# A hybrid decoder layer on one core: attention moved from the GLU into the out projection, low operands first, and a longer run of weight loads in the down stage

## The chip, the cores and the metric

The kernel runs on one core of a Trainium2 chip. The metric is the device time of one execution in microseconds, taken as the median of several runs. One further execution is profiled; the views of the profile and of its trace all describe that one.

## What is computed

One decoder layer on 256 tokens of width 2048, all in float32. One input projection feeds two groups; their results, side by side, go through one output projection, a norm, a gated feed-forward net and a second norm:

```python
proj = h @ w_in[l]
u_ssm, q, k, v, qi, ki, wi = jnp.split(proj, split_at, axis=-1)
...
y_attn = _dsa_attention(q, k, v, qi, ki, wi)
mix = jnp.concatenate([y_ssm.astype(h.dtype), y_attn.astype(h.dtype)], axis=-1) @ w_out[l]
h = _layer_norm(DEEPNORM_ALPHA * h + mix, ln1_g[l], ln1_b[l])
f = _conv_ffn(h, w_up[l], w_gate[l], conv_w[l], conv_b[l], w_down[l])
h = _layer_norm(DEEPNORM_ALPHA * h + f, ln2_g[l], ln2_b[l])
...
# the end of _s5_mixer, which gives y_ssm
return y * jax.nn.sigmoid(y @ w_glu + b_glu)
...
# in _conv_ffn, with h = x @ w_up and hp its padded copy
hc = conv_b + sum(conv_w[i] * hp[:, i:i + seq] for i in range(CONV_WIDTH))
return (jax.nn.gelu(hc, approximate=False) * (x @ w_gate)) @ w_down
```

`w_out` is 2048 x 2048, `w_up` and `w_gate` are 2048 x 5632, `w_down` is 5632 x 2048.

The attention has 8 query heads of 128 in two groups of four, each group with one key and value head. An indexer scores all earlier tokens for each query, and only the 64 best are attended; in the kernel this is a mask that is added to the scores. Tokens come in two blocks of 128, so a block has 128 or 256 keys to look at.

## The kernel before

**Products.** Each float32 operand is split into a high part, in the format fp32r, and a low rest. ACT copies a weight into `wh` (L133) and DVE subtracts to get `wl` (L136); `split` does the same for activations (L181, L182). A product is then three: high by high, low by high, high by low (`mm3`, L186 to L188). The up and gate products use `wide_half` (L206): high and low part of the activation stand side by side, so a pass with a high weight has 512 columns and one with a low weight 256.

**Weights.** The list `order` names all weight blocks in the order of their use; each is loaded as two halves of 128x1024 (512 KB). `load` sends a half on SP's queue into one of three `raw` buffers, `fetch` issues its two copies into one of four `wh` and four `wl` buffers, and `next_half` keeps `state["ahead"]` halves fetched ahead of the one in use (four as a rule). Halves that are listed in `special` have buffers of their own, so that the queue can run further ahead; they are used from the third column block of the out projection on (`halves_before_db2`) and for the last 20 halves of the down products (`spare2`).

**Order.** The program is written once; a scheduler places independent instructions, except in `manual_schedule` stretches, which keep the written order on the engines that they name. Generators that are registered with `add_bg` are advanced by `pump` after each product group, so their work is spread among the products. ACT's functions that need a table go through `in_turn` (L175), which keeps them in written order.

**Stages around the change**, with the times of the trace. The eight GLU tiles (24 products each, over 8 blocks of the contraction) run to 278 us. Each writes one of four PSUM banks (`o00` to `o11`), and ACT's sigmoid must read a bank before the fifth tile after it can be written. `attention(0)`, the first four heads, is pumped beside the last projections and the GLU: scores (L720), mask and scaling on DVE (L724), their maximum (L726), exponentials on ACT (L175), normalisation (L734), transposes on TensorE (L740), a copy on ACT (L743), the product with the values (L747), and a split. Scores, transposes and value products share two PSUM buffers, `misc`. `attention(1)` is pumped into the out projection.

The out projection contracts 16 blocks into four column blocks `db` of 512. Blocks 0 to 7 of `mix` come from the GLU, 8 to 11 from `attention(0)`, 12 to 15 from `attention(1)`. It takes `db` 0 and 1 with the first half of `mix`, then both with the second half, then `db` 2 whole; `db` 3 follows in a hand-written stretch with the first norm, whose 32 transposes (L875) stand among its products. The up and gate stage (44 tiles, products from 401.5 us) comes next, then the down stage: 44 row blocks `f`, two halves each, twelve products per half, into eight accumulators. The last five row blocks (LAG = 5) are collected and used column block by column block, so their ten halves must all be there; `state["ahead"]` is raised to ten at `f == NF - 2 * LAG`, f = 34. The activations of a row block are split just ahead of its use (`act_split`), with seven buffers.

Of the kernel before, what the change touches and what calls it, by code (L numbers as in the profile page):

```python
# [10 lines left out]
F32 = mybir.dt.float32  # L11
# [71 lines left out]
def block_kernel(ctx: ExitStack, tc: tile.TileContext, x_t, x_n, prm_d, cst_d, ssm_d, w_in_d, w_kw_d, w_v_d,  # L83
# [17 lines left out]
    order += [w_out_d[i] for i in (0, 1, 4, 5, 2, 3, 6, 7, 8, 9, 10, 11, 12, 13, 14, 15)]  # L101
# [5 lines left out]
    for n, src in enumerate(order):  # L107
        if n == 41:
            halves_before_db2 = len(halves)
        w = src.shape[1]  # L110
        halves += [src[:, :w // 2], src[:, w // 2:]]
# [82 lines left out]
    def wide_half(out, half, tiles, kh):  # L194
# [7 lines left out]
        steps = list(passes(0)) + list(passes(1))  # L202
        if kh:
            steps.append(steps.pop(7))
# [501 lines left out]


    def attention(c):
        qs = qt[4 * c:4 * c + 4]
        for b in range(2):  # L710
            w = 128 * (b + 1)
            e4 = post.tile([P, 4, S], F32, name="e4", bufs=2)
            mx = post.tile([P, 4], F32, name="mx", bufs=2)
            sm = post.tile([P, 4], F32, name="sm", bufs=2)
            nh = 512 // w
            for g0 in range(0, 4, nh):
                lp = misc_tile()
                for g in range(g0, g0 + nh):
                    o = lp[:, (g - g0) * w:(g - g0 + 1) * w]
                    T.matmul(o, lhsT=qs[g][:, b * 128:(b + 1) * 128], rhs=kt_[c][:, 0:w], start=True, stop=True)  # L720
                    yield
                for g in range(g0, g0 + nh):
                    hd = c * 4 + g
                    V.scalar_tensor_tensor(e4[:, g, :w], lp[:, (g - g0) * w:(g - g0 + 1) * w], SCALE * 2.0 ** (hd + 1),  # L724
                                           nm[b][:, :w], op0=ALU.mult, op1=ALU.add)
            V.tensor_reduce(mx, e4[:, :, :w], axis=AX.X, op=ALU.max)  # L726
            V.tensor_tensor(mx, mx, cc("nslope")[:, c * 4:c * 4 + 4], op=ALU.mult)
            for g in range(4):
                in_turn(e4[:, g, :w], e4[:, g, :w], AF.Exp, scale=2.0 ** -(c * 4 + g + 1), bias=mx[:, g:g + 1],
                             accum_out=sm[:, g:g + 1])  # L730
            rs = post.tile([P, 4], F32, name="rs", bufs=2)
            V.reciprocal(rs, sm)
            for g in range(4):
                V.tensor_scalar(e4[:, g, :w], e4[:, g, :w], rs[:, g:g + 1], None, op0=ALU.mult)  # L734
            yield
            pt = []
            for sb in range(b + 1):
                tp = misc_tile()
                for g in range(4):
                    T.transpose(tp[:, g * 128:(g + 1) * 128], e4[:, g, sb * 128:(sb + 1) * 128], ident)  # L740
                    yield
                t = post.tile([P, 512], F32, name="pt", bufs=3)
                A.activation(t, tp, AF.Copy)  # L743
                pt.append(t)
# [478 lines left out]
```

## Time and profile before

| | |
|---|---|
| three runs | 1144.85, 1138.44, 1144.31 us (median 1144.31) |
| profiled execution, device time | 1139.62 us |
| its span in the profile | 1137.8 us, mean granted clock 0.984 |
| PE (matmul) busy | 1097.6 us, 96% |
| DVE busy | 748.2 us, 66% |
| ACT busy | 563.7 us, 50% |
| weights read | 200 MB, 178 GB/s over the span |

Engines are PE (TensorE), DVE (VectorE), ACT (ScalarE), POOL and SP, whose queue issues the loads. Times count from the start of the span. The granted clock is the share of TensorE's 2.4 GHz that it was allowed to run at: 1.00 is full, 0.50 is 1.2 GHz.

### The profile page before, as it was taken

The numbers are of one execution on the slowest core, as the hardware profiler recorded it, in microseconds if no ns is written. First come the engines' busy times: TensorE is split into PE (matmuls) and PEld (weight loads), VectorE is DVE, ScalarE is ACT, GpSimd is POOL, SyncE is SP. The second block draws the span as 40 slices with busy tenths as digits, with TensorE's granted clock in tenths as the row PEclk, the third lists the DMA queues.
The fourth block names the chain that finished last, engine by engine and source line by source line (L and its number), as shares of the span: only waits on it lengthen the run. The fifth ranks groups of instructions, "written<-read, shape, count | busy, mean of one in ns | idle before, by whom it ended". The sixth has DMA issues, their size and how long they took to land.

```text
span 1137.8 us, 16797 instructions
## 1 busy us (share of the span) xinstructions
PE 1097.6 (96%) x6576; PEld 945.3 (83%) x6576; DVE 748.2 (66%) x1052; ACT 563.7 (50%) x813; POOL 0.2 (0%) x4
## 2 busy tenths in 40 slices
PE   8999999877999999999999999999999999999975
PEld 7998999767878888888888888888888888888864
DVE  7979998785666756677666565666565544444557
ACT  5865436445554755555444555545555444444430
POOL 0000000000000000000000000000000000000000
PEclk9999999988999999999999999999999999999988
DMA  8753444323566375555755555555554655555632
GB/s 267 237 167 115 159 145 145 139 74 108 207 212 214 104 259 192 185 185 187 262 194 190 189 189 187 192 187 187 185 188 165 216 189 186 186 188 190 212 130 74
DMA packets 59310, 204.44 MB, mean 180 GB/s; under 512 B 7264, under 2 KB 10080, under 8 KB 58592
## 3 DMA queue, kind: packets, MB, share of 16 engines
q1 hardware_dynamic: 59232, 203.38, 52.8%
q8 instruction: 51, 0.84, 0.3%
q14 instruction: 27, 0.22, 0.1%
HBM read 200.20 MB, written 2.10 MB: 178 GB/s over the span
## 4 chain that ended last, share of the span: by engine, by line
PE 86%; DMA 6%; DVE 3%; ACT 2%; issue 1%; SPq 1%; DVEq 0%; ACTq 0%
PE pd L206 41%; PE e L186 6%; PE e L188 6%; PE e L187 6%; PE acc L188 4%; PE acc L186 4%; PE acc L187 4%; DMA raw<-in_w_down_dram 3%; PE o L188 3%; PE o L187 3%; PE o L186 3%; DMA raw<-in_w_in_dram 1%; PE misc L599 1%; PE bu L556 1%; DVE wl L136 1%
## 5 line engine op out<-in xcount | busy, mean ns | idle before, releaser
L136 DVE TENSOR_TENSOR wl<-raw,wh 128x1024 fp32r<-128x1024 f32 x333 | 406.8, 1223 | 309.9 <-ACT wh L133 308.5
L133 ACT ACTIVATE wh<-raw 128x1024 fp32r<-128x1024 f32 x333 | 352.1, 1058 | 339.4 <-PE pd L206 141.5
L206 PE MATMUL pd<-mix,wh 128*128 128x512 f32 x1344 | 337.7, 393 | 0.7 <-ACT gate L1005 0.7
L206 PEld LDWEIGHTS pd<-mix,wh 128*128 128x128 f32 x1344 | 241.5, 189 | 44.0 <-ACT gate L1005 1.1
L206 PEld LDWEIGHTS pd<-mix,wl 128*128 128x128 f32 x1344 | 183.3, 190 | 13.1
L206 PE MATMUL pd<-mix,wl 128*128 128x256 f32 x1344 | 187.4, 282 | 0.0
L186 PE MATMUL e<-wh,acth 128*128 128x512 f32 x304 | 120.6, 397 | 5.5 <-ACT wh L133 5.5
L187 PE MATMUL e<-wh,actl 128*128 128x512 f32 x304 | 120.3, 396 | 0.0
L188 PE MATMUL e<-wl,acth 128*128 128x512 f32 x304 | 119.6, 396 | 0.5 <-DVE wl L136 0.5
L186 PE MATMUL acc<-x,wh 128*128 128x256 f32 (+1 forms) x400 | 113.9, 285 | 1.4 <-ACT x L181 1.2
L187 PE MATMUL acc<-x,wl 128*128 128x256 f32 (+1 forms) x400 | 114.2, 286 | 0.7 <-DVE wl L136 0.5
L188 PE MATMUL acc<-x,wh 128*128 128x256 f32 (+1 forms) x400 | 114.1, 285 | 0.8 <-DVE x L182 0.8
L186 PEld LDWEIGHTS acc<-x,wh 128*128 128x128 f32 (+1 forms) x400 | 75.8, 190 | 3.1 <-ACT x L181 1.4
L187 PEld LDWEIGHTS acc<-x,wl 128*128 128x128 f32 (+1 forms) x400 | 75.8, 190 | 2.2 <-DVE wl L136 0.7
L188 PEld LDWEIGHTS acc<-x,wh 128*128 128x128 f32 (+1 forms) x400 | 75.9, 190 | 2.1 <-DVE x L182 1.0
L186 PEld LDWEIGHTS e<-wh,acth 128*128 128x128 f32 x304 | 57.1, 188 | 20.0 <-ACT wh L133 6.2
L188 PEld LDWEIGHTS e<-wl,acth 128*128 128x128 f32 x304 | 57.1, 188 | 15.0 <-DVE wl L136 1.0
L187 PEld LDWEIGHTS e<-wh,actl 128*128 128x128 f32 x304 | 57.1, 188 | 13.8
L175 ACT ACTIVATE hc<-hc 128x256 f32<-128x256 f32 x44 | 18.4, 417 | 69.8 <-DVE hc L1046 69.8
L1033 DVE TENSOR_TENSOR sum<-sum,pd 128x256 f32<-128x256 f32 x84 | 34.9, 415 | 0.0
L188 PE MATMUL o<-wl,mix 128*128 128x512 f32 x80 | 31.9, 398 | 0.0
L186 PE MATMUL o<-wh,mix 128*128 128x512 f32 x80 | 31.6, 397 | 0.0
(262 smaller groups left out, 1201.7 us busy)
## 6 DMA issues: line engine op xcount, KB each, us to landing
raw<-in_w_gate_dram SPq DMA_DIRECT2D x88, 512.0 KB, 4.1
raw<-in_w_up_dram SPq DMA_DIRECT2D x88, 512.0 KB, 4.1
raw<-in_w_down_dram SPq DMA_DIRECT2D x88, 512.0 KB, 3.7
raw<-in_w_in_dram SPq DMA_DIRECT2D x51, 512.0 KB, 4.1
raw<-in_w_out_dram SPq DMA_DIRECT2D x32, 512.0 KB, 4.6
raw<-in_w_glu_dram SPq DMA_DIRECT2D x8, 512.0 KB, 3.8
raw<-in_w_v_dram SPq DMA_DIRECT2D x4, 512.0 KB, 4.5
z<-in_x_n_dram SPq DMA_DIRECT2D x1, 2048.0 KB, 8.8
```

The costliest lines, as they stand in the source:

```text
L133: A.activation(h[:, :w], raw[:, :w], AF.Copy)
L136: V.tensor_sub(l[:, :w], raw[:, :w], h[:, :w].bitcast(F32))
L175: ins = A.activation(*args, **kw)
L186: T.matmul(out, lhsT=lh[0], rhs=rh[0], start=start, stop=False)
L187: T.matmul(out, lhsT=lh[1], rhs=rh[0], start=False, stop=False)
L188: return T.matmul(out, lhsT=lh[0], rhs=rh[1], start=False, stop=stop).ins
L206: ins = T.matmul(out[:, 0] if low else out, lhsT=w, rhs=r, start=kh == 0 and i == 0, stop=kh == 1 and i == 15)
L556: T.matmul(bu[:, sd, ri, k:k + 128], lhsT=bt[r, 2 * bi + c_, h, ri, :], rhs=ustk[r, c_, h, :], start=True, stop=True)
L599: T.matmul(yp[32 * q:32 * q + 32, c_, e, k1:], lhsT=cbd[k1 * 2 + ri][:, ct * 4 + q, :], rhs=hv[ri][:, q % 2, k:k + 128 - k1], start=False, ...
L1033: V.tensor_tensor(t, t, p[:, 0], op=ALU.add)
```

## The change

There are three parts.

*GLU first.* `attention(0)` leaves the background of the GLU. The attention is now a class with four steps: `scores`, `weights` (exponentials, reciprocal, normalisation), `turn` (transposes and their copies) and `values` (products with the values, and the split into `mix`), and there are four chains: `a00` and `a10` for the first token block of either group of heads, `a01` and `a11` for the second. Only the scores of `a00` and `a10` stand among the GLU tiles; the first two GLU tiles are interleaved. The out projection takes three column blocks at once, in three phases over the contraction, so 24 units (a unit is the six products of one half with one token block) come ahead of the first that reads an attention result. TensorE's order there is written by hand: the table `beside` says ahead of which unit each step of the attention stands. The third column block accumulates in two banks that are free then.

*Low operands.* In `wide_half`, the second half of each tile takes its eight low passes first and its eight high passes after them.

*Ten buffers through down.* The queue may run ten halves ahead from f = 4 on. Special buffers are listed for the last 80 halves; two of each ten live in `hl2` and `hl3`, four in a new pool. The activations are split in groups of four row blocks into `hl0` and `hl1`.

```diff
-    order += [w_out_d[i] for i in (0, 1, 4, 5, 2, 3, 6, 7, 8, 9, 10, 11, 12, 13, 14, 15)]
+    order += [w_out_d[i] for i in (0, 1, 4, 5, 8, 9, 2, 6, 10, 3, 7, 11, 12, 13, 14, 15)]
...
-        steps = list(passes(0)) + list(passes(1))
-        if kh:
-            steps.append(steps.pop(7))
+        steps = list(passes(1)) + list(passes(0)) if kh else list(passes(0)) + list(passes(1))
...
+    class Attend:
+        def scores(self):
...
+            self.e4 = e4 = post.tile([P, 4, w], F32, name=f"e4{b}", bufs=2)
+            self.mx = mx = post.tile([P, 4], F32, name="mx", bufs=4)
...
+        def weights(self):
...
+        def turn(self):
...
+        def values(self):
...
+    a00, a10, a01, a11 = (Attend(c, b) for b in range(2) for c in range(2))
...
-    def beside_q():
-        yield from glu_in()
-        yield from attention(0)
-
-    add_bg(beside_q(), 1)
+    add_bg(glu_in(), 1)
...
+    first_glu = [(glu_acc(nt), next_half()) for nt in range(2)]
+    for some in (range(6), range(6, 8)):
+        for acc, half in first_glu:
+            glu_products(acc, half, some)
+    for nt in range(8):
...
+        sgm = post.tile([P, S], F32, name="sgm", bufs=2)
+        in_turn(sgm, acc[:, :S], AF.Sigmoid, bias=pc("bglu", nt))
...
+        if nt == 3:
+            a00.scores()
+        if nt == 4:
+            a10.scores()
...
-    add_bg(attention(1), 2)
...
-                t = post.tile([P, 4, 128], F32, name="h1f", bufs=2)
+                t = post.tile([P, 4, 128], F32, name="h1f", tag="pt", bufs=3)
...
-    for db, some in ((0, range(4)), (1, range(4)), (0, range(4, 8)), (1, range(4, 8)), (2, range(8))):
...
+    oacc = [row_banks(0), row_banks(1), [acc_tile() for _ in range(2)], None]
+    a00.weights()
+    a10.weights()
+    beside = {2: a01.scores, 3: a01.weights, 6: a00.turn, 7: a10.turn, 9: a00.values, 10: a10.values,
+              11: a11.scores, 12: a11.weights, 14: a01.turn, 17: a01.values, 22: a11.turn, 25: a11.values}
+    unit = 0
+    with tc.manual_schedule(engines={mybir.EngineType.PE}):
+        for some in (range(4), range(4, 6), range(6, 8)):
...
+            for db in range(3):
+                for i in some:
+                    half = next_half()
+                    for b in range(2):
+                        beside.get(unit, lambda: None)()
+                        rows_half(oacc[db][b], mix, 2 * i, half, b, 16)
+                        unit += 1
...
-        if i < 4:
+        if i < 2:
...
-    for i in range(4 * LAG):
+    for i in range(16 * LAG):
         if i % (2 * LAG) < 2 * LAG - 4:
-            special[len(halves) - 4 * LAG + i] = spare2(i % (2 * LAG))
+            special[len(halves) - 16 * LAG + i] = spare2(i % (2 * LAG))
...
     def act_split(f):
-        h = ff.tile([P, S], F32R, name="acth", bufs=LAG + 2)
-        l = ff.tile([P, S], F32R, name="actl", bufs=LAG + 2)
+        if f < 1:
+            h, l = (ff.tile([P, S], F32R, name=f"act{n}{f}") for n in "hl")
+        else:
+            slot, place = (f - 1) // 4, (f - 1) % 4
+            if place == 0:
+                parts[slot] = ahl.tile([P, 4, 2, S], F32R, name="acthl", tag=f"hl{slot % 2}")
+            h, l = (parts[slot][:, place, i] for i in range(2))
...
-        if f == NF - 2 * LAG:
+        if f == NF - 8 * LAG:
             state["ahead"] = 2 * LAG
```

Where this moves instructions, engine by engine. ACT in the later part of the GLU, before: weight copies (`wh`), the softmax of the second token block (`e4` by exponentials, with `sm` their sums) and the first sigmoid (`sgm`), which reads the accumulator `glu`.

```order
L133 ACTIVATE wh_3005<-raw_3003 128x1024
L133 ACTIVATE wh_3041<-raw_3039 128x1024
L743 ACTIVATE pt_2703<-misc_2678 128x512
L133 ACTIVATE wh_3077<-raw_3075 128x1024
L181 ACTIVATE mixh_2572<-misc_2705 128x4x128
L175 ACTIVATE e4_2715,sm_2717<-e4_2715,mx_2716 128x256 x4
L175 ACT_TABLE_LOAD
L175 ACTIVATE sgm_2961<-glu_2930,prm_70 128x256
```

The same place in the changed kernel:

```order
L133 ACTIVATE wh_3011<-raw_3009 128x1024
L133 ACTIVATE wh_3060<-raw_3058 128x1024
L175 ACTIVATE sgm_2954<-glu_2923,prm_70 128x256
L175 ACTIVATE sgm_2990<-glu_2959,prm_70 128x256
L133 ACTIVATE wh_3096<-raw_3094 128x1024
L133 ACTIVATE wh_3132<-raw_3130 128x1024
L181 ACTIVATE mix0_2847<-sgm_2954 128x256
L181 ACTIVATE mix0_2847<-sgm_2990 128x256
L133 ACTIVATE wh_3210<-raw_3208 128x1024
L175 ACTIVATE sgm_3039<-glu_3008,prm_70 128x256
```

The exponentials no longer stand ahead of the sigmoids; the third sigmoid (`sgm_2954`) now stands behind the weight copy `wh_3060`, and the fifth (`sgm_3039`) behind `wh_3210`.

DVE at the end of the attention's second block, before: maximum `mx`, reciprocal `rs` and normalisation of `e4`, then the sigmoids' products with y (`sgm`, L790) and their splits (`mix0`).

```order
L726 TENSOR_REDUCE mx_2716<-e4_2715 128x4
L727 TENSOR_TENSOR mx_2716<-mx_2716,cst_71 128x4
L732 RECIPROCAL rs_2746<-sm_2717 128x4
L734 TENSOR_SCALAR e4_2715<-e4_2715,rs_2746 128x256 x4
L790 TENSOR_TENSOR sgm_2961<-sgm_2961,y0_1087 128x256
L790 TENSOR_TENSOR sgm_2997<-sgm_2997,y1_1089 128x256
L182 TENSOR_TENSOR mix0_2926<-sgm_2961,mix0_2926 128x256
```

In the changed kernel DVE comes to the first normalisations at the start of the out projection (`e41` are scores of the second token block, `e40` the weights of the first; `mix1` the last GLU splits):

```order
L721 SCALAR_TENSOR_TENSOR e41_3232<-misc_3234,nm1_1901 128x256 x2
L721 SCALAR_TENSOR_TENSOR e41_3232<-misc_3239,nm1_1901 128x256 x2
L733 RECIPROCAL rs_3189<-sm_3184 128x4
L723 TENSOR_REDUCE mx_3233<-e41_3232 128x4
L733 RECIPROCAL rs_3200<-sm_3195 128x4
L735 TENSOR_SCALAR e40_2995<-e40_2995,rs_3189 128x128 x4
L182 TENSOR_TENSOR mix1_2848<-sgm_3124,mix1_2848 128x256
L182 TENSOR_TENSOR mix1_2848<-sgm_3160,mix1_2848 128x256
L724 TENSOR_TENSOR mx_3233<-mx_3233,cst_71 128x4
L735 TENSOR_SCALAR e40_3044<-e40_3044,rs_3200 128x128 x4
```

The scores of the second block and the last two products of the GLU now stand ahead of the first normalisation, and both reciprocals stand ahead of it too.

ACT toward the end of the down stage, before: a weight copy for each half and the split `acth` of one row block after about every second copy; the special buffers `wx` begin here.

```order
L133 ACTIVATE wh_9772<-raw_9770 128x1024
L133 ACTIVATE wh_9794<-raw_9792 128x1024
L181 ACTIVATE acth_10056<-act_4203 128x256
L133 ACTIVATE wh_9812<-raw_9810 128x1024
L133 ACTIVATE wx_9852<-raw_9850 128x1024
L133 ACTIVATE wh_9834<-raw_9832 128x1024
L181 ACTIVATE acth_10096<-act_4203 128x256
L133 ACTIVATE wx_9873<-raw_9871 128x1024
L133 ACTIVATE wx_9890<-raw_9888 128x1024
L181 ACTIVATE acth_10136<-act_4203 128x256
L133 ACTIVATE wx_9911<-raw_9909 128x1024
```

ACT in the same stage of the changed kernel:

```order
L181 ACTIVATE acthl_9840<-act_4209 128x256 x4
L133 ACTIVATE wx_9712<-raw_9710 128x1024
L133 ACTIVATE wx_9731<-raw_9729 128x1024
L133 ACTIVATE wxh2_9748<-raw_9746 128x1024
L133 ACTIVATE wxh3_9768<-raw_9766 128x1024
L133 ACTIVATE wxh4_9786<-raw_9784 128x1024
L133 ACTIVATE wxh5_9806<-raw_9804 128x1024
L133 ACTIVATE wh_9824<-raw_9822 128x1024
L133 ACTIVATE wh_9845<-raw_9843 128x1024
L181 ACTIVATE acthl_9991<-act_4209 128x256 x4
```

The splits stand in groups of four (`acthl`), and eight weight copies, six of them into special buffers, stand between two groups.

## Rows read from the trace of the kernel before

**Rows 1.** The page: busy time of each engine; shares of the last chain.

```profile
PE 1097.6 (96%) x6576; PEld 945.3 (83%) x6576; DVE 748.2 (66%) x1052; ACT 563.7 (50%) x813; POOL 0.2 (0%) x4
...
PE 86%; DMA 6%; DVE 3%; ACT 2%; issue 1%; SPq 1%; DVEq 0%; ACTq 0%
```

**Rows 2.** Windows: length, busy PE, PEld, DVE, ACT, POOL, granted clock, DMA share, GB/s.

```profile
240.00:260.00 20.00, 9.11 (x58) 7.25 (x56) 16.09 (x43) 9.38 (x21) 0.00 (x0) 0.82 0.30 105
370.00:392.00 22.00, 21.93 (x111) 17.66 (x111) 17.16 (x33) 17.28 (x37) 0.00 (x0) 1.00 0.34 117
1080.00:1100.00 20.00, 13.98 (x57) 10.46 (x56) 10.68 (x11) 9.25 (x11) 0.00 (x0) 0.89 0.56 187
```

**Rows 3.** PE's waits in 200 to 330: us in total, times, longest.

```profile
PE glu L186 <- ACT sgm L175: 9.9, 1, 9.9
...
PE misc L720 <- DVE mixl L182: 2.0, 1, 2.0
```

**Rows 4.** Timeline of ACT around 240 to 262: start, us, what, idle before.

```profile
240.96 1.06 ACT L133 ACTIVATE wh<-raw 128x1024 fp32r<-128x1024 f32 x1 [3.95 <-PE glu L188]
242.03 1.28 ACT L175 ACT_TABLE_LOAD   x1
...
243.73 0.39 ACT L175 ACTIVATE e<-e,mx 128x128 f32<-128x128 f32 x1
...
258.54 0.51 ACT L175 ACTIVATE e<-e,mx 128x256 f32<-128x256 f32 x1 [9.37 <-DVE mx L727]
...
261.93 0.47 ACT L175 ACTIVATE sgm<-glu,prm 128x256 f32<-128x256 f32 x1
```

**Rows 5.** Windows through the first hole.

```profile
245.00:252.50 7.50, 4.03 (x16) 2.29 (x14) 7.41 (x20) 3.91 (x5) 0.00 (x0) 1.00 0.50 175
252.50:262.50 10.00, 0.13 (x2) 0.04 (x1) 7.01 (x21) 3.93 (x11) 0.00 (x0) 0.51 0.16 59
262.50:266.30 3.80, 3.80 (x18) 3.80 (x19) 3.09 (x8) 2.67 (x7) 0.00 (x0) 0.50 0.00 0
```

**Rows 6.** PE's waits in 1040 to 1130.

```profile
PE e L186 <- ACT wh L133: 5.5, 2, 4.8
```

**Rows 7.** The last chain in 1040 to 1137.8: start, us, piece.

```profile
1052.41 1.24 DVE wx L136
...
1067.09 3.64 DMA raw<-in_w_down_dram
...
1073.16 6.95 DMA raw<-in_w_down_dram
```

**Rows 8.** Windows through the second hole.

```profile
1092.00:1099.60 7.60, 1.58 (x6) 0.51 (x4) 3.15 (x4) 3.11 (x3) 0.00 (x0) 0.74 0.62 208
1099.60:1102.50 2.90, 2.90 (x7) 2.33 (x8) 2.41 (x2) 1.06 (x1) 0.00 (x0) 0.50 0.00 0
```

**Rows 9.** Timeline of PE from the last GLU products to the first out products.

```profile
277.71 0.28 PE L188 MATMUL glu<-yl,wh 128*128 128x256 f32 x1
...
278.06 0.28 PE L188 MATMUL glu<-yl,wh 128*128 128x256 f32 x1
278.18 0.39 PE L186 MATMUL o<-wh,mix 128*128 128x512 f32 x1
278.41 0.40 PE L187 MATMUL o<-wh,mix 128*128 128x512 f32 x1
```

**Rows 10.** Timeline of DVE around 245.

```profile
245.49 0.86 DVE L734 TENSOR_SCALAR e<-e,rs 128x128 f32<-128x128 f32 x4
```

**Rows 11.** The page, DMA issues: count, KB each, median us to landing.

```profile
raw<-in_w_down_dram SPq DMA_DIRECT2D x88, 512.0 KB, 3.7
...
raw<-in_w_out_dram SPq DMA_DIRECT2D x32, 512.0 KB, 4.6
...
z<-in_x_n_dram SPq DMA_DIRECT2D x1, 2048.0 KB, 8.8
```

**Rows 12.** Groups of instructions by line and form, PE in 237 to 402.

```profile
L875 PE MATMUL misc<-cst,z 128*128 128x128 f32 x32 | 4.6, 275 | 0.1
```

More of the change, by code (lines that the diff above doesn't have):

```diff
@@ L107, in block_kernel @@
     for n, src in enumerate(order):
-        if n == 41:
-            halves_before_db2 = len(halves)
+        if n == 42:
+            halves_before_spare = len(halves)
         w = src.shape[1]
@@ L704, in block_kernel, with __init__ @@
     post = pre.enter_context(pool("post"))
[L708 to L714, printed above, removed]
+    class Attend:
+        def __init__(self, c, b):
+            self.c, self.b, self.w = c, b, 128 * (b + 1)
+        def scores(self):
+            c, b, w = self.c, self.b, self.w
+            self.e4 = e4 = post.tile([P, 4, w], F32, name=f"e4{b}", bufs=2)
+            self.mx = mx = post.tile([P, 4], F32, name="mx", bufs=4)
             nh = 512 // w
@@ L894, in spare @@
                 lambda: proj.tile([P, 1024], F32R, name="wql", tag=("qi1", "q1")[n]))
-    first = halves_before_db2
-    for i in range(24):
+    first = halves_before_spare
+    for i in range(22):
         if i % 11 < 7:
             special[first + i] = spare(i)
-    oacc = {}
     def rows_half(out, tiles, kt0, half, b, n):
@@ L913, in row_banks @@
         return [pso.tile([P, 512], F32, name=f"o{i}{b}") for b in range(2)]
-    for db, some in ((0, range(4)), (1, range(4)), (0, range(4, 8)), (1, range(4, 8)), (2, range(8))):
-        if 4 in some:
-            drain()
-            if db == 0:
+    oacc = [row_banks(0), row_banks(1), [acc_tile() for _ in range(2)], None]
[6 more added lines that the diff above has]
+        for some in (range(4), range(4, 6), range(6, 8)):
+            if 6 in some:
                 root_ready(post)
@@ L923, in block_kernel @@
                     nc.sync.dma_start(out=ln10[:, i], in_=ln_d[i:i + 1, :512].broadcast_to([P, 512]))
-        if db == 2:
-            state["ahead"] = 10
-        if some[0] == 0:
-            oacc[db] = row_banks(db % 2)
-        for i in some:
-            half = next_half()
-            for b in range(2):
-                rows_half(oacc[db][b], mix, 2 * i, half, b, 16)
-        if 7 in some:
-            for b in range(2):
-                residual(b, db, oacc[db][b])
+                state["ahead"] = 10
+            for db in range(3):
[5 more added lines that the diff above has]
+                        unit += 1
+                if 7 in some:
+                    for b in range(2):
+                        residual(b, db, oacc[db][b])
     oacc[3], gacc = row_banks(1), row_banks(0)
@@ L1008, in block_kernel @@
     pre.close()
+    wx2 = ctx.enter_context(pool("wx2"))
     ff = ctx.enter_context(pool("ff"))
```

68 lines of the change are left out of this document (33 added, 35 removed).

## Prediction

> **What bounds the kernel now.** The page comes first. TensorE is busy 96% of the span, and 86% of the chain that ended last is its own work [rows 1]. A gain must therefore come from stretches in which TensorE has nothing to do or runs at the lower of its two clocks. Windows of some 20 us find them: 9.1 us busy at a granted clock of 0.82 in 240 to 260, 14.0 at 0.89 in 1080 to 1100, while a window in the middle, 370 to 392, is full at 1.00 [rows 2]. That is the whole case: two holes and a dense rest.
>
> The list of waits names what ends the first hole: 9.9 us for a sigmoid, and before it 2.0 for a split of the attention [rows 3]. The timeline of ACT says why. After the attention's last copy ACT stands idle for 9.37 us, until DVE has the scores' maximum; the exponentials run at 258.54, and the first sigmoid of the GLU waits behind them until 261.93 [rows 4]. The fifth GLU tile needs the PSUM bank which that sigmoid reads. Narrow windows size the hole: 4.03 of 7.5 us busy, then 0.13 of 10, which is 13.3 us idle, and behind it 3.8 us of GLU products at a clock of 0.50 [rows 5], which cost 1.9. **First hole: 13.3 + 1.9 = 15.2 us.**
>
> The second hole is a wait for `wh` in the down products, 5.5 us [rows 6]. The chain there alternates between landings of `w_down` halves and their two copies [rows 7]: ten halves are wanted almost at once for the last five row blocks, and the queue had only ten row blocks to run ahead. Windows give 1.58 us busy of 7.6, then 2.9 us of products at 0.50 [rows 8], which cost 1.45. **Second hole: 6.0 + 1.45 = 7.45 us.**
>
> **The change part by part.** *GLU first.* Up to 237.1 TensorE's list is the same; from there the attention of the first head group no longer stands inside the GLU. No product is added or removed: its 68 products still run, now inside the out projection. So all that changes is waiting, and I count the waits that the new lists make, with durations of before. A GLU product (256 columns) starts every 0.117 us (three in 0.35), an out product (512) every 0.23 [rows 9], so a GLU tile of 24 takes 2.8 us and one unit (six products of a half with one token block) 1.4. The parts of the walk: `wh` copy 1.06, table load 1.28, exponentials 0.39 each, sigmoid 0.47 [rows 4], `wl` 1.24 [rows 7], normalisation of four heads 0.86 [rows 10].
>
> Wait 1. The first four sigmoids no longer wait for an exponential: `wh` of the fifth tile starts at 240.96 as before, the table is in at 243.3, the first sigmoid done at 243.8. The fifth and sixth tile find their banks free; 109 of their products are left at 237.1 (12.8 us), eight score products stand among them (0.9), and they end at 250.8. The seventh needs the third sigmoid, which ACT holds behind `wh_3060`. That copy's load is sent when the sixth tile's `wl` is done: `wh` at 244.8, `wl` at 246.0, then 3.7 to 4.6 us of landing [rows 11], 1.06 and 0.47. The sigmoid is done at 251.3 to 252.1: wait 0.5 to 1.3, I take 0.9.
>
> Wait 2. The first out product writes the bank of the fifth tile, whose sigmoid ACT holds behind `wh_3210`. That copy takes the buffer of the eighth tile, so it starts only when the GLU ends. 1.06 + 0.47 and two hand-overs: 1.7 (bounds 1.5 and 2.0).
>
> Wait 3. `a00.turn` stands six units and one set of scores (0.9) after the first out product: 9.3 us. ACT has by then `wh_3228`, which waits two units for its buffer (2.8 + 1.06), two sigmoids (0.9), the table (1.28) and eight exponentials (3.1): 9.2. DVE takes both reciprocals ahead of the first normalisation (0.86): 10.4 with hand-overs. Wait 1.1 (bounds 0, since the units may start late, and 2.3, one more `wl`).
>
> Wait 4. `a11.scores` stands one unit behind `a10.values`, and its second tile takes the PSUM buffer that the split of those values must leave. In before the same pair cost 2.0 [rows 3]; bounds 0 and 2.0, I take 0.5, as a whole unit now lies between. The other places (turns at units 14 and 22, values at 9, 10, 17, 25) have three units or more behind their softmax, and wait 0.
>
> Sum of new waits 4.2 us; the clock should hold, none being near the 9.9 that preceded the fall. **First hole: 15.2 − 4.2 = 11.0 us gained.**
>
> *Three column blocks.* 24 units lie ahead of the first one that reads the attention (unit 24), 33 us; the weights arrive in the new order of the list, as many as before. One half serves 2.8 us. A raw buffer is held for a landing of 4.6 [rows 11] and two copies of 1.06 and 1.24, with three buffers 2.3 us per half, so it is covered; if that cover were gone, each half would cost 4.1 (9 to 15 halves until the spare buffers start). Loading `z` (8.8 us to landing [rows 11]) stands on SP's queue ahead of the sixth out half, which is wanted 14 us after; hidden.
>
> *Low operands.* In the second half of each up or gate tile the eight low passes go before the eight high ones. A pass costs what its own columns cost, whichever came before: 0.117 us between two of 256 columns, 0.12 from one of 256 to one of 512, 0.23 behind that [rows 9]. The sum does not change: 0 us, with 84 tiles and a border worth at most 0.02 us each way, ±1.7. `wl` of an odd half is wanted 1.6 us sooner; four buffers of 2.8 us cover that.
>
> *Ten buffers through down.* The queue may run ten halves ahead from f = 4, not from f = 34. One half is used in 2.8 us (twelve products), while a raw buffer's round is 3.64 + 1.06 + 1.24 at best, 2.0 us per half with three of them [rows 4, 7]. Six halves of lead (16.8 us) need about 21 halves at a gain of 0.8; there are 70. The activations now take `hl0` and `hl1` in groups of four: each group waits for the group two before it, on ACT ahead of the weight copies. Only the first groups press: `hl0` is read last 2.8 us before the up stage ends, and f = 1 is wanted 5.6 us after, 8.4 us for at most seven splits of under 0.5 (a sigmoid of the same 128x256 takes 0.47). Nothing waits: **7.45 us gained**. The range of this term is 0 to 7.45.
>
> Sum: 11.0 + 7.45 = 18.5 us, from the profiled execution's 1139.6 to 1121.1. Of the runs shown two lie at about 1144.5 and one at 1138.4, so the profiled one is 4.7 under the median; the same gain from the median gives 1125.8, from the lowest run 1120. I say 1122.
>
> **The rivals.** *Late at set places.* TensorE's list is fixed in the out projection, so any late softmax blocks the products behind it. In 245 to 252.5 three waits of the attention cost 3.5 us [rows 5], 1.15 each; if six more places wait so, that is 6.9 us, and one more fall of the clock 1.9: 1130. For it: DVE is 7.41 of 7.5 us busy there [rows 5]. Against: it has 33 us for that work.
>
> *Loads do not get ahead.* At the end of before a landing took 6.95 us [rows 7]; with the copies that is 9.3, 3.1 us per half with three buffers, and the lead never grows. The second hole stays: 1128.6. Against: the median landing of `w_down` is 3.7 [rows 11].
>
> *Nothing waits.* All four new waits vanish, since the lists absorb them: 1139.6 − 22.7 = 1117.
>
> *Slower.* TensorE drops to 1.2 GHz among the set places and stays. A product then takes 0.41 us (seven in 2.9 [rows 8]), not 0.23: 1.1 us per unit. Twenty-six units reach to the last set place; at 17 of them the gain of 18.5 is gone, and at 26 the time is 1121 + 28 = 1149. For it: the clock fell twice behind waits (to 0.51 in 252.5 to 262.5 [rows 5], 0.74 on average in 1092 to 1099.6 [rows 8]). Against: in 370 to 392, where the norm turns its rows by fp32 transposes among the products, the clock is 1.00 [rows 2, 12]. The Trainium skill bears on this: "TensorE: Matmul & The Clock Gate", section "Part 4: PE-mode transpose", says that transposes do not count as activity for the clock, which would put the stretch with the turns at the lower level; the trace of the norm's 32 transposes does not agree, so I leave this case a small chance.
>
> **How the numbers follow.** Forecast (1117.5 to 1127) 0.62, nothing waits 0.10, late at set places 0.13, loads not ahead 0.05, slower 0.04, both holes half left (about 1136) 0.06. The range leaves out the last two and reaches from 1117 less the spread of a run and the 1.7 of the borders, 1113, to 1130 plus 3 for a run near the median, 1133. About 1% is what a measurement here can tell from no change, so the bound is 1133: faster 0.84, same 0.12, slower 0.04.
>
> **What would show it.** Right: no wait of TensorE over 2.5 us between 237 and 300, the first up product near 390 instead of 401.5, the pause of down gone, the interval of up products unchanged. Wrong: a wait for `e40` or `e41` of several us, a granted clock below 1.00 between 250 and 300, or `wh` waits in the last five row blocks.

## The result, and the profile after

| | before | changed |
|---|---|---|
| runs | 1144.85, 1138.44, 1144.31, 1140.73 us | 1111.4, 1112.53, 1108.79, 1110.82 us |
| median | 1142.52 us | 1111.11 us |
| span of the profiled execution | 1137.8 us | 1109.5 us |

The ratio is 0.9727, with a 95% interval of 0.9691 to 0.9763: faster by some 31 us, where 20 were forecast (1122 against 1142.5), and below the lower end of the range, 1113. The two profiled executions differ by 28.3 us, where 18.5 were worked out. The direction was right; the size was not.

The first thing to do with such a miss is to split it by stage. These times are read from the starts and ends of the products in the two traces:

| stage | before | changed | difference | forecast |
|---|---|---|---|---|
| to the first GLU product (same program) | 228.55 | 231.19 | +2.64 | 0 |
| first GLU product to first up product | 172.94 | 158.42 | −14.52 | −11.0 |
| up and gate, to the first down product | 470.32 | 468.74 | −1.58 | 0 |
| down, to the end of the last product | 254.50 | 239.67 | −14.83 | −7.45 |
| last norm and store | 11.51 | 11.52 | 0 | 0 |

The first line is scatter: over the thirteen profiled executions of this study, with the same order of TensorE's work up to there, the first GLU product starts between 228.55 and 234.12. So the miss lies in the down stage above all.

The page of the changed kernel, as [rows 1] of before:

```profile
PE 1084.8 (98%) x6576; PEld 944.1 (85%) x6576; DVE 747.0 (67%) x1052; ACT 561.0 (51%) x812; POOL 0.2 (0%) x4
...
PE 93%; DMA 2%; DVE 2%; ACT 1%; SPq 1%; issue 1%; DVEq 0%; ACTq 0%
```

TensorE went from 96 to 98% of the span, which is the two holes. But its busy time also fell, from 1097.6 to 1084.8 us, with the same 6576 products. Idle time that goes can't do that. The two stretches at the lower clock behind the holes, which are gone too, explain 3.3 us of the 12.8 [rows 5, 8]; for the rest, the products themselves take less.

The changed kernel's longest waits after the first GLU product, over the whole span (in total, times, longest), to be laid beside [rows 3, 6]:

```profile
PE o L186 <- ACT sgm L175: 2.6, 1, 2.6
...
PE pd L204 <- ACT gate L1021: 0.7, 1, 0.7
PE misc L887 <- issue: 0.6, 1, 0.6
```

The 9.9 for a sigmoid and the 5.5 for `wh` are gone. Of the four new waits one is there, the second. The windows around it (length, busy PE, PEld, DVE, ACT, POOL, granted clock, DMA share, GB/s), beside [rows 5]:

```profile
245.00:259.40 14.40, 14.40 (x123) 14.20 (x122) 13.71 (x33) 9.54 (x15) 0.00 (x0) 1.00 0.55 182
259.40:262.03 2.63, 0.00 (x0) 0.00 (x1) 1.96 (x5) 1.47 (x3) 0.00 (x0) 1.00 0.79 238
262.03:268.03 6.00, 6.00 (x27) 5.05 (x28) 5.59 (x15) 4.29 (x8) 0.00 (x0) 1.00 0.88 337
262.10:275.00 12.90, 12.90 (x61) 10.78 (x62) 12.10 (x35) 11.19 (x32) 0.00 (x0) 1.00 0.70 277
```

The GLU runs without a gap, then 2.63 us are idle, then all is dense at full clock, the turns included.

Now the down stage, in a window where neither kernel waits: before, then changed.

```profile
900.00:1000.00 100.00, 100.00 (x430) 80.31 (x429) 50.08 (x54) 43.47 (x54) 0.00 (x0) 1.00 0.54 189
```

```profile
900.00:1000.00 100.00, 100.00 (x443) 82.81 (x442) 58.06 (x63) 50.66 (x63) 0.00 (x0) 1.00 0.67 223
```

Both are busy for all of 100 us at a clock of 1.00, yet one starts 430 products and the other 443. The timelines of PE show the same over twelve products each, before and then changed:

```profile
900.03 0.39 PE L187 MATMUL e<-wh,actl 128*128 128x512 f32 x1
...
902.83 0.39 PE L187 MATMUL e<-wh,actl 128*128 128x512 f32 x1
```

```profile
900.21 0.39 PE L187 MATMUL e<-wh,acthl 128*128 128x512 f32 x1
...
902.93 0.39 PE L187 MATMUL e<-wh,acthl 128*128 128x512 f32 x1
```

2.80 us against 2.72, so 0.2333 us a product against 0.2267. Over the 1056 products of the stage that is about 7 us, nearly the whole miss of this stage (14.83 against 7.45). "0.23 us" in the prediction had rounded this away.

A clue to its cause is in the changed kernel itself. Its 24 products of the first row block, whose activations lie in a buffer of their own, start every 0.233 us; from the second row block on, with `acthl` in `hl0` and `hl1`, it is 0.227. The built program says where each buffer lies. Before, the split activations lie 224 bytes further, modulo 512, than the weight buffers `wh` and `wl`; `acthl` lies at the same place modulo 512. In each pair of products the one reads its moving operand (the weights here) while the stationary operand of the next (the activations) is loaded, as the busy PEld beside the busy PE shows. That gave the theory of the experiments: the interval hangs on the distance of these two.

### The profile page after: what moved, and what is told of

It is laid out like the page before. It is cut to its first block, busy times and chain, and to the rows that moved or that the text cites. A ratio compares the mean times of both kernels' runs of the same rounds, so it can differ in the third digit from the quotient of the medians.

```text
span 1109.5 us, 16801 instructions
## 1 busy us (share of the span) xinstructions
PE 1084.8 (98%) x6576; PEld 944.1 (85%) x6576; DVE 747.0 (67%) x1052; ACT 561.0 (51%) x812; POOL 0.2 (0%) x4
## 4 chain that ended last, share of the span: by engine, by line
PE 93%; DMA 2%; DVE 2%; ACT 1%; SPq 1%; issue 1%; DVEq 0%; ACTq 0%
PE pd L204 42%; PE e L186 7%; PE e L188 7%; PE e L187 7%; PE acc L188 5%; PE acc L186 5%; PE acc L187 5%; PE o L186 3%; PE o L188 3%; PE o L187 3%; PE misc L653 1%; PE misc L597 1%; PE bu L554 1%; DVE wl L136 1%; DMA xraw<-in_x_t_dram 1%
## 5 line engine op out<-in xcount | busy, mean ns | idle before, releaser
L136 DVE TENSOR_TENSOR wl<-raw,wh 128x1024 fp32r<-128x1024 f32 x299 | 364.7, 1221 | 247.6 <-ACT wh L133 244.1
L133 ACT ACTIVATE wh<-raw 128x1024 fp32r<-128x1024 f32 x299 | 315.7, 1057 | 271.8 <-PE pd L204 136.3
L204 PE MATMUL pd<-mix,wh 128*128 128x512 f32 x1344 | 321.4, 391 | 0.7 <-ACT gate L1021 0.7
L204 PE MATMUL pd<-mix,wl 128*128 128x256 f32 x1344 | 174.8, 283 | 0.0
L136 DVE TENSOR_TENSOR wxl<-raw,wxh 128x1024 fp32r<-128x1024 f32 x42 | 51.4, 1225 | 43.9 <-ACT wxh L133 42.3
L133 ACT ACTIVATE wxh<-raw 128x1024 fp32r<-128x1024 f32 x42 | 44.6, 1061 | 54.3 <-DMA raw<-in_w_down_dram 20.4
L187 PE MATMUL e<-wh,acthl 128*128 128x512 f32 x152 | 59.1, 389 | 0.0
L186 PE MATMUL e<-wh,acthl 128*128 128x512 f32 x152 | 59.0, 389 | 0.0
L188 PE MATMUL e<-wl,acthl 128*128 128x512 f32 x152 | 58.3, 389 | 0.0
L186 PE MATMUL e<-wxh,acthl 128*128 128x512 f32 x128 | 49.8, 389 | 0.0
L187 PE MATMUL e<-wxh,acthl 128*128 128x512 f32 x128 | 49.8, 389 | 0.0
L188 PE MATMUL e<-wxl,acthl 128*128 128x512 f32 x128 | 49.8, 389 | 0.0
```

What stands on the lines that cost most here:

```text
L133: A.activation(h[:, :w], raw[:, :w], AF.Copy)
L136: V.tensor_sub(l[:, :w], raw[:, :w], h[:, :w].bitcast(F32))
L186: T.matmul(out, lhsT=lh[0], rhs=rh[0], start=start, stop=False)
L187: T.matmul(out, lhsT=lh[1], rhs=rh[0], start=False, stop=False)
L188: return T.matmul(out, lhsT=lh[0], rhs=rh[1], start=False, stop=stop).ins
L204: ins = T.matmul(out[:, 0] if low else out, lhsT=w, rhs=r, start=kh == 0 and i == 0, stop=kh == 1 and i == 15)
```

## Experiments

**Each part alone.** The first three runs take the parts of the change apart. The first is the changed kernel with the old `wide_half` and the old down stage (`spare2`, its list and `act_split` as before):

```diff
-        steps = list(passes(1)) + list(passes(0)) if kh else list(passes(0)) + list(passes(1))
+        steps = list(passes(0)) + list(passes(1))
+        if kh:
+            steps.append(steps.pop(7))
...
-        if f == NF - 8 * LAG:
+        if f == NF - 2 * LAG:
```

> The first part of the change alone: the kernel before with the GLU first and the attention in four chains, the up, gate and down stages as before. Theory (the three parts add up, each in its own stage): from the first GLU product to the first up product 158.4 us as in the changed kernel, against 172.9 before, so 13 to 14.5 us less, near 1126; the down products still start every 0.2333 us on average and still pause for about 6 us near the end. Rival (the down stage is shorter because the stages ahead of it end earlier or leave the buffers free sooner): the down stage shrinks from 254.5 us here as well.

Measured: 1125.85 us (median of 4), ratio 0.987 [0.9839, 0.9901]. First GLU product to first up product 159.2 us, down stage 252.8, up and gate 470.3. The down products keep their old interval and wait once, in the list of PE's waits:

```profile
PE e L186 <- ACT wh L133: 3.6, 1, 3.6
```

So the attention's part acts in its own stage alone; that the products of down come closer together because of earlier stages is ruled out. The pause itself differs between executions: by the starts of the products, the waits and the stretch at the lower clock behind them cost 8.2 us in the profiled before, 6.5 here and 6.2 in the next run, which has the old down stage too. The stage from the first GLU product to the first up product took 171.2 to 172.9 us in the five executions with the old attention (mean 171.9), and 158.4 to 161.7 in the five with the new lists as they are (mean 159.7). That is 12 us, with the single pair 14.5, where 11.0 were forecast.

The second part alone, in the kernel before:

```diff
-        steps = list(passes(0)) + list(passes(1))
-        if kh:
-            steps.append(steps.pop(7))
+        steps = list(passes(1)) + list(passes(0)) if kh else list(passes(0)) + list(passes(1))
```

> The second part alone: low passes first in the second half of each up or gate tile. Theory (a change from low to high passes costs products that start late, and a tile now has one such change instead of two): the sum of the 32 intervals of a tile goes from 5.587 us to 5.567, 1.7 us over 84 tiles, with the five intervals behind a low pass at 0.233, 0.236, 0.228, 0.233 and 0.231 us and the others at 0.227. Rival (the 1.6 us by which the up stage of the changed kernel is shorter come from other placements of its buffers): the sum stays at 5.587.

Measured: 1137.0 us, one run, inside the 1136.0 to 1142.35 of the runs of before beside it, so the time alone shows nothing. The trace does. The up and gate stage took 468.7 us instead of 470.3, and a tile 5.567 instead of 5.587. The intervals of a tile, read from the starts in the trace (mean over 76 tiles, us):

```
                              before                       low passes first in the second half
first half, 8 high            .2358 .2283 .2325 .2308      .2267 x8
                              .2267 x4
            8 low             .1133 .1192 .1200 x6         .1133 .1192 .1200 x6
second half                   .2333 .2358 .2283 .2325      8 low:  .1200 x8
                              .2308 .2267 x2 (7 high)      8 high: .2333 .2358 .2283 .2325
                              .1133 .1192 .1200 x6 (low)           .2308 .2267 x3
                              .2333 (1 high)
```

A high pass behind a low one opens five late intervals, 0.027 us together; a low pass behind a high one gives 0.008 back. Before, each tile has two of either, now one. 0.020 us by 84 tiles is 1.7.

The third part with its new places undone:

```diff
-    for i in range(4 * LAG):
+    for i in range(16 * LAG):
         if i % (2 * LAG) < 2 * LAG - 4:
-            special[len(halves) - 4 * LAG + i] = spare2(i % (2 * LAG))
+            special[len(halves) - 16 * LAG + i] = spare2(i % (2 * LAG))
...
-        if f == NF - 2 * LAG:
+        if f == NF - 8 * LAG:
```

> The third part without its new places: the kernel before, with the queue ten halves ahead from the fourth row block on and the list of special buffers over the last 80 halves; the split activations and the special buffers stay where they were. Theory (two things shortened the down stage: the pause, and the interval of the products, which hangs on where the split activations lie): the pause goes, the interval stays at 0.2333 us, the down stage takes 254.5 - 7.45 = 247 us and the kernel 7 to 8 us less. Rival (the loads that run further ahead make the products start closer together): interval 0.2267, the down stage 240 us, 14 to 15 us less.

Measured: 1130.13 us, ratio 0.9919 [0.9888, 0.9949]. No wait of TensorE is left in the down stage, and it took 245.6 us: 8.9 less than the profiled before, 7.7 less than the mean of the three executions with the old down stage (254.5, 252.8, 252.6). Of either, 0.7 us comes from the products that start sooner, the rest is the pause. The window of 900 to 1000, beside the two above:

```profile
900.00:1000.00 100.00, 100.00 (x433) 80.74 (x432) 56.06 (x59) 49.61 (x61) 0.00 (x0) 1.00 0.66 218
```

433 products, not 443: loads that run ahead do not bring the products closer. The three above 430 come from the halves in the two special buffers that lie in the activations' own pool, at distance 0; behind six products of that kind the interval is 0.2269, and with the other halves 0.2333.

**The place of the activations alone.** Before with one unused piece of memory, nothing else:

```diff
+    ff.tile([P, 72], F32, name="shift")
+
     def act_split(f):
```

> The kernel before with one unused piece of 288 bytes ahead of the buffers of the split activations and nothing else. It moves them, and two of the special weight buffers, from 288 bytes above a multiple of 512 to 64 above one, which is where the weight buffers lie. Theory (a product starts later when the stationary operand that is loaded next and the moving operand that is read meanwhile lie at different places modulo 512 bytes): the down products start every 0.2267 us instead of 0.2333, the stage takes 6.9 us less, the pause stays. Rivals (that high and low part share one tile, or lie in the region of the old activations, or that the loads run ahead): no change, 254.5 us for the stage.

Measured: 1132.9 us, ratio 0.9952 [0.9925, 0.9979]. The same window:

```profile
900.00:1000.00 100.00, 100.00 (x443) 82.81 (x442) 51.30 (x56) 44.43 (x55) 0.00 (x0) 1.00 0.60 195
```

443, as in the changed kernel, with the old buffers, the old run of loads and two tiles for high and low part. The stage takes 245.4 us, and the pause is still there, though shorter:

```profile
PE e L186 <- ACT wh L133: 2.7, 2, 2.2
PE e L188 <- DVE wl L136: 0.5, 1, 0.5
```

Of the 9.1 us that the stage is shorter than in the profiled before, 2.4 are this shorter pause (5.8 us with its lower clock, against 8.2) and 6.7 the interval. This settles that the place makes the interval. The kernel gained 6.8 us by the medians from 288 bytes that nobody writes.

**Which distance counts.** Seven buffers at seven distances:

```diff
-        h = ff.tile([P, S], F32R, name="acth", bufs=LAG + 2)
-        l = ff.tile([P, S], F32R, name="actl", bufs=LAG + 2)
+        s = f % 7
+        if f < 7:
+            ff.tile([P, (288, 32, 32, 64, 64, 64, 128)[s] // 4], F32, name=f"shift{s}")
+        h = ff.tile([P, S], F32R, name=f"acth{s}x", bufs=1)
+        l = ff.tile([P, S], F32R, name=f"actl{s}x", bufs=1)
```

> The kernel before with a buffer of its own for the activations of every seventh row block of the down stage, at seven distances from the weight buffers: 0, 32, 64, 128, 192, 256 and 384 bytes modulo 512 (high and low part alike). Theory (only the same place modulo 512 is fast): row blocks of the first distance have products every 0.2267 us, all others 0.2333. Rivals: the same place modulo 256 (then 256 is fast as well), modulo 128 (then 128, 256 and 384 too), or modulo 64 (then all but 32). The mean over the seven tells how many are fast: 0.2323, 0.2314, 0.2295 and 0.2276 us in this order.

Measured: 1137.2 us, one run. The mean interval of the down products by distance, behind at least six products at the same distance (so that late intervals of a change of place are left out):

```
distance, bytes modulo 512     0     32     64    128    192    256    384
products                     101     84    107    108     90     90     90
interval, us               .2267  .2333  .2333  .2320  .2289  .2267  .2327
```

The theory was wrong in its modulus: 256 is as good as 0. The values between are not all alike, and 192 lies between the two levels. What stays is 0 modulo 256, among the distances tried; why 256 is not shown.

**Another stage, another operand.** If the distance counts, moving all activations against the weights must cost in the up stage too, where the activation is the moving operand.

```diff
+    gap = ctx.enter_context(pool("gap"))
+    gap.tile([P, 64], F32, name="shift")
     ahl = ctx.enter_context(pool("ahl"))
```

> The changed kernel with an unused piece of 256 bytes ahead of the pool that holds the activations of every stage. They all move by 256 against `wh` and `wl`; the special buffers of the down stage, which lie behind that pool, move with them. Theory (the distance modulo 512 counts, in every stage): down products with a half in `wh` or `wl` start every 0.2333 us, those with a half in a special buffer every 0.2267, in the same stage; up and gate products, whose moving operand is the activation, gain up to 16 times 0.0067 us a tile, 9 us over the stage (5.567 to 5.67 us a tile); the kernel gets 9 to 15 us slower than the changed one, near 1122. Rival (only the stage with split activations as stationary operand minds, or 256 is as good as 0): the up stage stays at 5.567 us a tile, and the time within 4 us of 1111.

> The changed kernel with an unused piece of 32 bytes, not 256, ahead of the pool that holds the activations of every stage. Seven places and the shift by 256 left a distance of 0 modulo 256 as the fast one. Theory (that distance counts for every product of 512 columns, whichever operand is the activation): down products with a half in `wh` or `wl` start every 0.2333 us and those with a half in a special buffer every 0.2267 (456 and 576 of 1032, so 3.0 us more for the stage); the up and gate stage, all of whose halves lie in `wh` and `wl`, goes from 5.567 us a tile to at most 5.67, up to 9 us more; the kernel lies near 1123. Rival (it counts only where the activation is the stationary operand): the down stage is 3.0 us longer, the up stage stays, the kernel lies near 1114.

Measured: 1114.62 us with 256 bytes, 1117.77 with 32 (the same edit with `[P, 8]`), where 1122 and 1123 were expected. The windows of the up stage and of the down stage, first the changed kernel's up stage, then both with 256 bytes, then both with 32:

```profile
500.00:800.00 300.00, 300.00 (x1726) 265.08 (x1725) 186.41 (x249) 152.76 (x216) 0.00 (x0) 1.00 0.59 197
```

```profile
500.00:800.00 300.00, 300.00 (x1726) 265.09 (x1726) 186.15 (x250) 153.29 (x216) 0.00 (x0) 1.00 0.61 196
900.00:1000.00 100.00, 100.00 (x443) 82.81 (x442) 58.15 (x63) 50.60 (x62) 0.00 (x0) 1.00 0.67 223
```

```profile
500.00:800.00 300.00, 300.00 (x1719) 260.83 (x1718) 186.65 (x249) 152.13 (x215) 0.00 (x0) 1.00 0.60 195
900.00:1000.00 100.00, 100.00 (x436) 81.68 (x436) 55.64 (x58) 48.00 (x57) 0.00 (x0) 1.00 0.66 218
```

With 256 bytes nothing moves in either stage (the changed kernel has 1726 and 443), which fits the seven places and refutes what I expected of that run; both stages take the same in the two profiled executions (468.7 and 239.7 us), and the 3.5 us between the medians are less than the changed kernel's own runs differ by (1108.79 to 1117.78). With 32 both stages slow down. The down stage is 3.3 us longer (3.0 expected): its products with `wh` and `wl` take 0.2333, those with the special buffers, which moved along, 0.2267, with the activations at one and the same place for both. So the distance counts, and not the place of the activations by itself. In the up stage the high passes take 0.2333 on average, whichever came before, as the theory says, but the low passes fall from 0.120 to 0.117, so that a tile costs 5.600, not 5.67, and the stage 2.7 us, not up to 9. So the distance counts whichever operand is the activation; for passes of 256 columns it does something else, which stays open.

That the moving operand is to be compared with the stationary operand of the next product, not with its own, is seen where a distance of 0 goes over into one of 32. In the seven places the stationary operand changes its place there, and the very first interval is late: 0.235 us, the mean of five such changes. In the run with 32 bytes the moving operand changes its place instead; the first interval is still 0.227, and the second is 0.234, the mean of seven.

**The wait that is left.** Ahead of the first out product the changed kernel's ACT does this (timeline: start, us, what, idle before):

```profile
257.64 1.06 ACT L133 ACTIVATE wh<-raw 128x1024 fp32r<-128x1024 f32 x1 [1.87 <-DMA raw<-in_w_out_dram]
...
260.56 1.06 ACT L133 ACTIVATE wh<-raw 128x1024 fp32r<-128x1024 f32 x1 [1.24 <-DMA raw<-in_w_out_dram]
261.52 0.82 ACT L175 ACTIVATE sgm<-glu,prm 128x256 f32<-128x256 f32 x2
```

The fifth sigmoid stands behind a copy, as the prediction said, but the copy waits for its load, not for its buffer, hence 2.6 us and not 1.7. Can it be had back?

```diff
-        in_turn(sgm, acc[:, :S], AF.Sigmoid, bias=pc("bglu", nt))
+        with tc.high_priority():
+            in_turn(sgm, acc[:, :S], AF.Sigmoid, bias=pc("bglu", nt))
```

> The changed kernel with the GLU's sigmoids issued at high priority, as the weight copies are. Theory (the one wait that is left ahead of the first out product, 2.6 us, is a sigmoid that stands on ACT behind a copy whose load has not landed): that wait goes or falls under 1 us, and GLU to first up product takes 156 to 157 us instead of 158.4. Rival (the first out product would have waited for its weight half anyway, which lands at 260.5): the wait stays near 2.6 us, but for `wh` or `wl`.

Measured: 1111.23 us, and 158.7 us from GLU to up: nothing gained. PE's timeline says where it went:

```profile
259.45 0.50 PE L186 MATMUL o<-wh,mix 128*128 128x512 f32 x1 [0.48 <-ACT sgm L175]
261.37 0.50 PE L186 MATMUL o<-wh,mix 128*128 128x512 f32 x1 [0.26 <-ACT sgm L175]
270.52 0.33 PE L742 MATMUL misc<-cst,e 128*128 128x128 f32 x1 [0.32 <-DVE e L735]
271.05 0.72 PE L742 MATMUL misc<-cst,e 128*128 128x128 f32 x3 [0.20 <-DVE e L735]
273.57 0.92 PE L742 MATMUL misc<-cst,e 128*128 128x128 f32 x4 [0.42 <-DVE e L735]
```

The first wait fell to 0.48, and the turns now wait for the normalised weights, piece by piece. The first product behind the second turn stands at 274.24 here and at 274.25 in the changed kernel. This is the prediction's third wait, which the second had hidden; DVE (11.98 of 13 us busy in 262 to 275 here, 12.10 of 12.9 in the changed kernel) sets the pace. The step then was to move the turns as well:

```diff
-    beside = {2: a01.scores, 3: a01.weights, 6: a00.turn, 7: a10.turn, 9: a00.values, 10: a10.values,
-              11: a11.scores, 12: a11.weights, 14: a01.turn, 17: a01.values, 22: a11.turn, 25: a11.values}
+    beside = {2: a01.scores, 3: a01.weights, 8: a00.turn, 9: a10.turn, 11: a00.values, 12: a10.values,
+              13: a11.scores, 14: a11.weights, 16: a01.turn, 19: a01.values, 22: a11.turn, 25: a11.values}
```

> The changed kernel with the sigmoids at high priority, as in the run before, and the turns, values and following steps of the attention two units later in the table (turns of the first block at units 8 and 9 instead of 6 and 7). Theory (with the sigmoid early, the units start 2.6 us sooner, but the normalised weights do not, so the turns took over the wait): two units, 2.7 us, cover it; GLU end to first up product 128 us instead of 130.2, the kernel 2 us under the changed one. Rival (the weight halves are late as well once the units start sooner): waits for `wh` or `wl` in the first ten units, and nothing gained.

Measured: 1111.75, 1110.75 and 1108.52 us, median 1110.75; a fourth execution took 2755.53 us, for a reason that stays open, and is not counted. GLU end to first up product 129.7 us, half a microsecond less than in the changed kernel instead of 2. No turn waits any more, but the out products do, 1.1 us for sigmoids and 0.3 for a split. DVE is about as loaded just behind the GLU as it was (13.04 of 14.6 us busy in 260.4 to 275, against 14.13 of 15.6 in 259.4 to 275 of the changed kernel). The last kernel adds the places of the buffers, by three unused pieces (128 bytes ahead of `mixh`, 224 ahead of `wxh`, 32 ahead of the first row block's activations), and ran beside the changed kernel:

> The kernel of the run before (sigmoids first, turns two units later) and three unused pieces (128, 224 and 32 bytes) that bring the attention's part of `mix`, the spare weight buffers of the out projection and the split activations of the first row block to the place of the weight buffers modulo 256. Theory: about 170 out products and 23 down products start 0.005 to 0.007 us sooner each, 1.1 us; with the 2 us of the moved turns about 3 us under the changed kernel, near 1108. Rival (the moves cost elsewhere or are lost in the scatter): within 1 us of the changed kernel.

> The changed kernel once more, beside the others and on the same chip, as the measure for the two before it: 1111 us, within 2 us.

Measured: 1110.28 us (1107.83 to 1111.08, ratio 0.9745 [0.9723, 0.9766]) against 1113.78 for the changed kernel (1108.94 to 1117.78, ratio 0.9776 [0.9748, 0.9804]). The intervals overlap, so it is not shown to be faster, and 1108 was expected; the changed kernel too lies further from its 1111 than the 2 us that I allowed. In the trace the 198 intervals of out products that the moved buffers bring to a distance of 0 or 256 went from 0.2334 to 0.2274 us, 1.2 us in all, but the wait at the norm's first transpose is 1.6 us, against 0.6 in the changed kernel's first profile, and takes most of it. The changed kernel's profiled execution of this call is worth a look, windows at the wait that is left:

```profile
260.97:263.79 2.82, 0.00 (x0) 0.00 (x0) 1.94 (x5) 1.47 (x3) 0.00 (x0) 0.89 0.57 173
263.79:269.50 5.71, 5.71 (x13) 4.46 (x14) 3.50 (x11) 1.76 (x4) 0.00 (x0) 0.50 0.90 366
```

After 2.82 us of waiting the clock was at its lower level for 5.7 us, 3 us lost; after 2.63 in the execution shown first, and after 2.7 to 3.2 in three other kernels with the same wait, it stayed at 1.00.

## Why the prediction was wrong

**What bounds the kernel** held: two holes in a dense rest, and both were filled, the first but for one wait.

**The first hole** held in place and, by the stage means, about in size. The gain by stage means was 12 us and in the profiled pair 14.5, for 11.0; the bounds of its four waits together (2.0 to 7.6 us) allowed 7.6 to 13.2, so the pair lies outside. Of the four new waits, the second came (2.6 for 1.7, with a load as its cause instead of a buffer), the third came out when the second was removed (0.94 us in three pieces, for 1.1), and the first and the fourth did not show. So the new waits were 2.6 us and not 4.2, which gives 15.2 − 2.6 = 12.6. The rest of the pair's 14.5 is partly the late start of the GLU: its first products run at the lower clock in both executions, and where it starts 2.6 us later fewer of them do (2.2 us at the lower clock instead of 3.6, which is 0.7 us gained); some 1.2 us stay open. The sign "no wait of TensorE over 2.5 us" was missed by 0.1: the wait is 2.63.

**Three column blocks** held: no wait for a weight half in the out projection, and the first up product stands at 389.6, for "near 390".

**Low operands** was mis-sized. The step "the sum does not change: 0 us" read the interval of a pass as its own columns' cost, from one border in [rows 9]. It is 1.6 to 1.7 us, since a change from low to high costs five late intervals. The bound of 1.7 happened to hold it.

**Ten buffers through down is the step that failed.** "Nothing waits: 7.45 us gained. The range of this term is 0 to 7.45" took the new places of the activations for a question of waits alone. The pause went, as the mechanism had it; it had cost 8.2 us in the profiled before, by the starts of the products. But `acthl` also came to lie at the place of the weight buffers modulo 256, so that 1032 products start every 0.2267 us, most of which had started every 0.2333. Over the 1044 intervals outside the pause that is 6.6 us, which no rival and no bound held; 8.2 and 6.6 are the 14.8 measured. With this term at 14.8 and low operands at 1.6 the sum would have been 11.0 + 1.6 + 14.8 = 27.4. That it comes so near to the 28.3 measured is in part luck: the first hole gave 3.5 us more in this pair than the term had, and the late start of the GLU took 2.6 back.

**The rivals.** Late at set places: no such waits in the changed kernel. Loads not ahead: refuted by the third run. Slower: the clock was 1.00 in the stretch with the turns, so the rule on transposes from the Trainium skill ("TensorE: Matmul & The Clock Gate", section "Part 4: PE-mode transpose") did not decide here, as in the norm before [rows 2, 12]; those transposes stand among many products, so it is not tested alone. Its milder form, a fall of the clock behind the one wait, happened in the changed kernel's second profiled execution and cost 3 us.

The "interval of up products unchanged", which I had named as a sign that the prediction is right, was the wrong sign: reading it to three digits in the trace of before (up 0.227 to 0.236, down 0.2333) would have put the question in time. The Trainium skill has it differently too: "SBUF — State Buffer", section "A bandwidth-pool intuition that's wrong (but worth ruling out)", gives TensorE a "2nd independent read port for LDWEIGHTS". By that, taken at its word, the place of the two operands would not matter; the seven places do not agree (0.2267 to 0.2333 us at the same clock and with the same products).

## What to carry to other kernels

In a stretch where TensorE is 100% busy at full clock, still divide the window by the count of products: 430 and 443 in 100 us look the same in PE's busy column, 100.00 in both. When a change moves a buffer, compare where stationary and moving operand lie, here modulo 256 bytes; it was worth nearly 7 us without a single wait. The wait that was removed here ahead of a loaded engine came back a few microseconds later, so look at what that engine owes next before counting the gain.

## What was not expected of the hardware

- A product of 512 columns (fp32r, in the down stage, at full clock) starts every 0.2267 us when the moving operand and the next stationary operand lie 0 or 256 bytes apart modulo 512, and every 0.2289 to 0.2333 at the other distances tried. Passes of 256 columns took 0.120 at distance 0 and 0.117 with a shift of 32.
- A break in the rhythm (a pass of 256 columns ahead of one of 512, at distance 0) costs five intervals of 0.233, 0.236, 0.228, 0.233 and 0.231 us before 0.2267 is reached again.
- The same wait of 2.6 to 3.2 us let the clock fall in one profiled execution of five. Why in that one stays open.
